# Two of the seven gate products of columns 0 to 255 placed beside the last recurrence, whose six units run in two groups of three

## The chip, the core and the metric

One core of one Trainium2 chip runs the whole program in one launch. The core has TensorE (PE; its weight loads are shown apart as PEld), VectorE (DVE), ScalarE (ACT), GpSimd (POOL) and SyncE (SP, which here only issues DMAs); 16 DMA engines move data between HBM and the on-chip memory. Time is the device time of one execution in microseconds (us); lower is better. The chip's time before is the median of three runs.

## The reference: what is computed

Two layers over 1152 tokens (1024 of one prompt, 8 times 16 of samples) of 1024 features. Layer 0 mixes tokens with an RWKV-7 recurrence, layer 1 with chunk-band attention; each is followed by a SwiGLU feed-forward network (FFN) with 2816 hidden features. Cut to what matters here:

```
mod = silu(c) @ w_ada + b_ada                    # shift, scale, gate of each sub-layer
h   = modulate(rms_norm(x, norm_mix), shift, scale)
y   = recurrence(r, w, k, v, a, b)               # per head, a 64x64 state, token after token
x   = x + gate * ((y_normed * g) @ w_o)          # output projection
h   = modulate(rms_norm(x, norm_ffn), shift, scale)
x   = x + gate * ((silu(h @ w_gate) * (h @ w_up)) @ w_down)
```

All matrices are float32. The kernel splits each float32 operand into a high and a low part and multiplies high by high, high by low and low by high, three matmuls in place of one.

## The kernel before, in words

**Layout.** Features lie on the 128 partitions, tokens along the free axis. The 1152 tokens are three blocks of 384 (b = 0, 1, 2) in layer 0's mixer and two column groups in the FFN: c = 0 is columns 0 to 511, c = 1 columns 512 to 1151.

**The mixer's stages.** The projections of block b run beside the recurrence of block b-1. The recurrence is cut into nine windows of 128 tokens, each in two halves of the heads (hf = 0, 1): 18 units. `win_prep` (L875) loads a unit's operands and forms its small products, `win_run` carries the state, `win_y` (L1065) and `win_post` (L1108) form, normalise and store its output. `windows` (L1192) takes the units in pairs: it prepares a pair, weaves the two state chains step by step, finishes both, prepares the next pair.

**The last recurrence.** In `layer0a` (L1271) the six units of windows 6, 7 and 8 run, in three pairs, beside a second stream, `early`: the output projection of block 0 (`outproj(0)`) in turn with the rest of the modulation vectors (`self.ada`, weights `in_wada`), then `outproj(1)`. Both load 128x1024 weight tiles named raw on POOL's DMA queue (L318), from a ring of two buffers here. An output projection has eight units, one for each row tile of 128 features: a raw tile of `in_rw_o` is split by ACT into whi (L330) and by DVE into wlo (L331), 24 matmuls of 384 columns go into the bank acc, and DVE adds the residual into e (L1228). Its block's rms is known after the eighth unit. The operand of a block, yg, is loaded and split into 16 mx tiles through mr, a ring of two. The windows' memory (pool `win`) is given back only after the last unit; the FFN's first buffers then take its place.

**The FFN of layer 0.** It forms gate and up together by a Strassen-Winograd scheme: for each of the 22 row tiles f of 128 hidden features, seven products (0, 1, 2, 4, 5, 6, 3 in this order) of 128x512 weight combinations with half of the features (512) of half of the columns of a group. `strassen_in` (L1344) makes the seven operands of a group: it loads x and the rms, normalises (L411, L412), combines (L1357), splits (L330, L331, tiles h). Products 0 and 1 are the gate weights as they are, times the two feature halves of the group's first columns: their sum is the plain gate of columns 0 to 255 (c = 0) and 512 to 831 (c = 1). `gate_up` (L1408): a product is 12 matmuls of 256 columns (c = 0) and 12 of 320 (c = 1) into one of three PSUM banks (S, S, PT); product 0 is copied to t1 by ACT (L1430), product 1 is added to it by DVE into s0, ACT takes Silu of s0 (L1432); products 2 and 4 are copied by ACT (L1433, L1434), and three additions of each f run on POOL (L1427 on POOL). t1 also enters the sums of product 5. The weight combinations are four POOL additions per f (L1398 to L1401), and POOL also adds down-projection weights (L1516 to L1519). Group c = 0 of f = 0 runs alone, then the operands of c = 1 are made, then c = 1 of f = 0, then f = 1 to 21 with both groups.

**What sets the order.** The program is written as interleaved generators; a scheduler with its own cost model then sets the order on every engine and queue before the launch. So each engine works through a fixed list, and what stands behind a waiting instruction on its engine waits too.

## Time and profile before

| what | us |
|---|---|
| median of three runs (lowest, highest) | 3768.5 (3764.55, 3778.86) |
| the profiled execution | 3766.23 |
| its span | 3764.4 |
| TensorE busy in the span | 3441.4 (91%) |
| output projection of block 0 with the modulation, from its first result to its last | 1023 to 1146 |
| output projection of block 1, first result to last | 1163 to 1200 |
| first result of the output projection of block 2 | 1247 |
| first f of the FFN with both groups | 1332 |

The page gives busy time by engine, then the span in 40 slices (each digit is a tenth; PEclk is the granted TensorE clock in tenths), then the chain of work that ended last, then groups of instructions. A matmul's duration there is that of one in flight; since they overlap, its price in a dense stretch is the distance between starts.

### The profile page before, as it was taken

Reading aid. Unit: us, or ns where it says so; the run is one execution under the profiler, and the core shown is the slowest. Engines: PE = TensorE matmul, PEld = TensorE weight load, DVE = VectorE, ACT = ScalarE, POOL = GpSimd, SP = SyncE. Lnnn points to the kernel's source line nnn. Section 1 sums busy time; section 2 is a strip of 40 time slices with the busy share of each in tenths; the row PEclk is TensorE's granted clock in tenths of the full one; section 3 lists DMA queues with packets and bytes.
Section 4 is the critical chain, followed back from the end, with each engine's and each line's share of the span. In section 5 each row is a group of like instructions: output and inputs, shape, how many; then the busy total and the mean of one; then the engine's idle time right before and its main releaser. Section 6 shows DMA issues by size and latency. Waiting matters only on the chain.

```text
span 3764.4 us, 74445 instructions
## 1 busy us (share of the span) xinstructions
PE 3441.4 (91%) x28982; PEld 3083.1 (82%) x28982; DVE 2248.7 (60%) x4366; ACT 1660.0 (44%) x3176; POOL 787.5 (21%) x775
## 2 busy tenths in 40 slices
PE   5888999999889799999999889789889899999999
PEld 4677778777667699999888869677667789999999
DVE  4667676765446765555446742666675675665655
ACT  5545556554223533333334542555564443333442
POOL 0000000000011066676100000000000146766200
PEclk9888899889699899999999999899999899999999
DMA  5776776677666444444889422445465434444764
GB/s 212 231 223 162 202 222 191 191 205 208 174 199 203 141 129 141 140 138 153 272 295 329 145 72 80 136 140 161 149 206 170 156 109 141 142 149 143 235 211 158
DMA packets 545938, 664.65 MB, mean 177 GB/s; under 512 B 137232, under 2 KB 405520, under 8 KB 541104
## 3 DMA queue, kind: packets, MB, share of 16 engines
q1 hardware_dynamic: 468736, 556.44, 46.5%
q0 software_dynamic: 23760, 85.08, 7.4%
q10 hardware_dynamic: 53088, 18.36, 2.1%
q8 instruction: 228, 3.74, 0.4%
q14 instruction: 126, 1.03, 0.1%
HBM read 483.18 MB, written 176.53 MB: 175 GB/s over the span
## 4 chain that ended last, share of the span: by engine, by line
PE 67%; DMA 13%; DVE 9%; issue 5%; ACT 4%; SPq 1%; POOL 1%; ACTq 0%; DVEq 0%; POOLq 0%
PE S L145 30%; PE PT L145 15%; PE acc L145 12%; PE st L145 3%; PE O L145 2%; PE G L145 1%; PE PT L2107 1%; PE aux L145 1%; DVE h L331 1%; PE Y L145 1%; DMA TT<-Z 1%; DMA raw<-in_wada 1%; DVE wlo L331 1%; DMA raw<-in_rw_o 1%; DMA aw<-in_wadb 1%
## 5 line engine op out<-in xcount | busy, mean ns | idle before, releaser
L145 PE MATMUL S<-h,w 128*128 128x256 f32 (+1 forms) x7374 | 1032.5, 299 | 24.8 <-ACT h L330 7.2
L145 PEld LDWEIGHTS S<-h,w 128*128 128x128 f32 x7374 | 1002.2, 191 | 43.2 <-issue 15.3
L330 ACT ACTIVATE w<-rq 128x512 fp32r<-128x512 f32 (+1 forms) x500 | 304.0, 614 | 645.8 <-PE S L145 259.6
L145 PE MATMUL acc<-mx,whi 128*128 128x384 f32 x1728 | 510.8, 373 | 31.6 <-ACT mx L330 12.3
L145 PE MATMUL PT<-h,w 128*128 128x256 f32 (+1 forms) x3714 | 527.4, 298 | 9.5 <-DVE h L331 3.5
L331 DVE TENSOR_TENSOR w<-rq,w 128x512 fp32r<-128x512 f32 (+1 forms) x500 | 384.7, 774 | 251.0 <-ACT w L330 212.6
L145 PEld LDWEIGHTS PT<-h,w 128*128 128x128 f32 x3714 | 505.3, 190 | 16.2 <-issue 6.5
L145 PEld LDWEIGHTS acc<-mx,whi 128*128 128x128 f32 x1728 | 339.7, 205 | 61.7 <-ACT mx L330 15.4
L145 PE MATMUL acc<-mx,wlo 128*128 128x384 f32 x864 | 318.0, 368 | 8.2 <-DVE wlo L331 8.2
L1427 POOL TENSOR_TENSOR t<-t,t 128x576 f32<-128x576 f32 (+1 forms) x132 | 221.9, 1683 | 263.0 <-ACT t L1434 153.3
L331 DVE TENSOR_TENSOR h<-h,h 128x1024 fp32r<-128x1024 f32 (+6 forms) x152 | 169.3, 1127 | 133.5 <-ACT h L330 120.6
L330 ACT ACTIVATE h<-h 128x1024 fp32r<-128x1024 f32 (+6 forms) x152 | 142.5, 950 | 158.8 <-DMA h<-bd 120.4
L145 PEld LDWEIGHTS acc<-mx,wlo 128*128 128x128 f32 x864 | 177.0, 205 | 19.7 <-DVE wlo L331 12.3
L331 DVE TENSOR_TENSOR wlo<-raw,whi 128x1024 fp32r<-128x1024 f32 x114 | 139.1, 1222 | 82.3 <-ACT whi L330 81.5
L330 ACT ACTIVATE whi<-raw 128x1024 fp32r<-128x1024 f32 x114 | 119.7, 1053 | 129.9 <-PE acc L145 73.0
L145 PE MATMUL S<-h,wh 128*128 128x320 f32 (+1 forms) x744 | 146.7, 351 | 19.5 <-ACT xo L1794 10.0
L145 PEld LDWEIGHTS S<-h,wh 128*128 128x128 f32 x744 | 123.6, 196 | 39.3 <-ACT xo L1794 15.8
L1427 DVE TENSOR_TENSOR t<-S,t 128x576 f32<-128x576 f32 (+1 forms) x117 | 86.7, 741 | 113.7 <-PE S L145 113.7
L145 PE MATMUL acc<-h,wh 128*128 128x256 f32 (+1 forms) x864 | 133.8, 303 | 3.5 <-DVE ht L391 1.3
L145 PEld LDWEIGHTS acc<-h,wh 128*128 128x128 f32 x864 | 118.0, 194 | 11.5 <-DVE ht L391 3.4
L1357 POOL TENSOR_TENSOR h<-h,h 128x256 f32<-128x256 f32 x12 | 10.7, 918 | 540.3 <-PE PT L145 540.3
L2108 ACT ACTIVATE pts<-PT 128x640 f32<-128x640 f32 (+4 forms) x128 | 72.6, 567 | 88.0 <-PE PT L2107 73.7
(480 smaller groups left out, 5536.4 us busy)
## 6 DMA issues: line engine op xcount, KB each, us to landing
bd<-t SPq DMA_DIRECT2D x154, 160.0 KB, 1.9
rq<-in_wg SPq DMA_DIRECT2D x88, 256.0 KB, 3.0
rq<-in_wu SPq DMA_DIRECT2D x88, 256.0 KB, 2.6
ws<-in_wd SPq DMA_DIRECT2D x64, 352.0 KB, 3.5
ws<-ws SPq DMA_DIRECT2D x64, 352.0 KB, 3.1
bd<-t SPq DMA_DIRECT2D x152, 128.0 KB, 1.8
rq<-ws SPq DMA_DIRECT2D x72, 256.0 KB, 3.2
h<-bd SPq DMA_DIRECT2D x28, 640.0 KB, 6.8
```

What stands on the lines that cost most here:

```text
L145: return nc.tensor.matmul(out, lhsT, rhs, start=start, stop=stop)
L330: self.nc.scalar.activation(hi, x, AF.Copy)
L331: self.nc.vector.tensor_tensor(lo, x, hi, ALU.subtract)
L1357: gp.tensor_tensor(out[j], x[j], y[j], op)
L1427: return eng.tensor_tensor(out, x, y, ALU.add)
L2107: nc.tensor.transpose(pt[:, j * 128:(j + 1) * 128], P[:, j * 128:(j + 1) * 128], self.C("ident"))
L2108: nc.scalar.activation(pts[:, 0:nk * 128], pt[:, 0:nk * 128], AF.Copy)
```

## The change

Products 0 and 1 of group c = 0 are computed earlier, beside the last recurrence, for all 22 f. `first_in` loads columns 0 to 255 of block 0's new x, normalises them with the rms that `outproj(0)` has just made, and splits them into eight high and eight low tiles, which lie in buffers that the recurrence no longer uses (pa, Aab, t11, p1, L, T, stmp, and a new one, op). `first_gates` loads the plain gate weights `in_wg0[f]` whole (128x1024, on POOL's queue), splits them, runs 24 matmuls of 256 columns in two halves of a bank acc, copies the first half by ACT, adds the second by DVE (L1310 in the changed kernel), and stores both, product 0 and the sum of 0 and 1, to gd in HBM. `gate_up` then loads those 256 columns of t1 and s0 from gd, and runs products 0 and 1 for the other 320 columns alone; `strassen_in` leaves out the splits of operands 0 and 1 of c = 0.

Beside this, the six units of the last recurrence run in two groups of three (12 13 16, then 14 15 17, as window and half in the base 2), the ring of raw has three buffers there in place of two, three steps of `early` are written for one of `windows` in place of two, the mix tiles are 384 wide in place of 408, and some operands of single units lie in other pools.

```diff
-        self.T = self.wp.tile([128, 16, 16], F32, name="T")
+        self.T = self.wt("T", [128, 16, 16])
...
-        ring, nr = (self.st, 1) if (w, hf) == (7, 1) and 1 else (self.wt, 3)
+        ring, nr = self.wt, 3
-        bk = self.wt("BK", [128, 8, 2, 64], 1)
+        bk = (self.st if (w, hf) in ((6, 1), (7, 0), (8, 1)) else self.wt)("BK", [128, 8, 2, 64], 1)
...
-    def windows(self, us):
+    def windows(self, us, n=2):
-        pairs = [us[i:i + 2] for i in range(0, len(us), 2)]
+        pairs = [us[i:i + n] for i in range(0, len(us), n)]
-                if u is run[0]:
+                if u is not run[-1]:
...
-            nc.sync.dma_start(self.rr[:, cols], self.sq_done(st))
+            self.rms = self.sq_done(st)
+            nc.sync.dma_start(self.rr[:, cols], self.rms)
...
+    def first_in(self):
+        wt = lambda tag, shape, bufs=1: self.wt(tag, shape, bufs, F32R)
+        p = wt("pa", [128, 2, 8, 64]).rearrange("p a b c -> p (a b c)")
+        t = [p[:, 256 * i:256 * i + 256] for i in range(4)]
+        for _ in range(2):
+            q = wt("Aab", [128, 8, 64], 2).rearrange("p a b -> p (a b)")
+            t += [q[:, 0:256], q[:, 256:512]]
+        t += [wt(f"{n}{h}", [128, 8, 32]).rearrange("p a b -> p (a b)") for n in ("t11", "p1") for h in range(2)]
+        t += [wt(n, [128, 16, 16]).rearrange("p a b -> p (a b)") for n in "LT"] + [wt("stmp", [128, 256])]
+        t.append(self.st("op", [128, 256], 1, F32R))
+        self.op = t[0:8], t[8:16]
+        self.Af0 = self.gain("nf0", 32)
+        for f in range(8):
+            x = self.mraw()[:, 0:256]
+            self.nc.sync.dma_start(x, self.x1[:, f, 0:256])
+            self.normed(x, self.rms[:, 0:256], self.Af0, 24, f)
+            self.split(self.op[0][f], self.op[1][f], x)
+            yield
+    def first_gates(self):
+        nc = self.nc
+        hi, lo = self.op
+        last = None
+        for f in range(22):
+            wh, wl = self.wunit(self.pp, self.a["wg0"][f])
+            if last:
+                nc.sync.dma_start(*last)
+            pz = self.bank("acc", 2)
+            t = self.st("gr", [128, 512], 3)
+            for h in range(2):
+                z = pz[:, 256 * h:256 * h + 256]
+                for k in range(4 * h, 4 * h + 4):
+                    s = slice(k * 128, (k + 1) * 128)
+                    self.mm3(z, wh[:, s], wl[:, s], hi[k], lo[k], k % 4 == 0, k % 4 == 3)
+                if h:
+                    nc.vector.tensor_tensor(t[:, 256:512], z, t[:, 0:256], ALU.add)
+                else:
+                    nc.scalar.activation(t[:, 0:256], z, AF.Copy)
+                yield
+            last = self.gd[:, f], t
+        nc.sync.dma_start(*last)
...
-        self.nraw, self.nhi, self.nlo = (2, 2, 2)
-        self.nmix, self.nmr = 16, 2
+        self.nraw, self.nhi, self.nlo = (3, 2, 2)
+        self.nmix, self.nmr, self.wmix = 16, 2, TB
         def early():
             yield from self.alternate(self.outproj(0), self.ada, 1, 1)
-            yield from self.outproj(1)
+            yield from self.first_in()
+            yield from self.alternate(self.outproj(1), self.first_gates(), 1, 2)
             self.last_in()
-        for _ in self.alternate(self.windows([divmod(int(x), 2) for x in '12 13 16 14 15 17'.split()]), early(), 1, 2):
+        for _ in self.alternate(self.windows([divmod(int(x), 2) for x in '12 13 16 14 15 17'.split()], 3), early(), 1, 3):
...
         def product(i):
             hi, lo = next(W)
+            ccs = [c for c in cs if c or not a or i > 1]
+            if not ccs:
+                return None
             t = self.wide()[:, 256:832]
-            for c in cs:
+            for c in ccs:
...
-        nc.scalar.activation(t1, product(0), AF.Copy)
-        add(dve, s0, product(1), t1)
+        if a:
+            nc.sync.dma_start(t1[:, 0:256], gd[:, 0:256])
+            nc.sync.dma_start(s0[:, 0:256], gd[:, 256:512])
+        z = product(0)
+        if n1 > a:
+            nc.scalar.activation(t1[:, a:], z[:, a:], AF.Copy)
+        z = product(1)
+        if n1 > a:
+            add(dve, s0[:, a:], z[:, a:], t1[:, a:])
```

In `gate_up`, `a` is 256 for layer 0 where group c = 0 takes part, and 0 elsewhere.

**How the order moves: POOL's DMA queue in the last recurrence.** Before, from the end of the first output projection on (raw is the ring, in_wada the modulation's weights, in_rw_o the output projection's):

```order
L318 DMA raw_12344<-in_rw_o 128x1024
L318 DMA raw_12360<-in_wada 128x1024
L318 DMA raw_12375<-in_wada 128x1024
L318 DMA raw_12566<-in_rw_o 128x1024
L318 DMA raw_12647<-in_rw_o 128x1024
L318 DMA raw_12814<-in_rw_o 128x1024
L318 DMA raw_12970<-in_rw_o 128x1024
```

Now, in the same place (in_wg is the gate weight of one f):

```order
L318 DMA raw_12197<-in_rw_o 128x1024
L318 DMA raw_12213<-in_wada 128x1024
L318 DMA raw_12233<-in_wada 128x1024
L318 DMA raw_12608<-in_rw_o 128x1024
L318 DMA raw_12624<-in_wg 128x1024
L318 DMA raw_12731<-in_wg 128x1024
L318 DMA raw_12909<-in_wg 128x1024
L318 DMA raw_12944<-in_rw_o 128x1024
L318 DMA raw_12960<-in_wg 128x1024
L318 DMA raw_13054<-in_wg 128x1024
L318 DMA raw_13153<-in_wg 128x1024
L318 DMA raw_13188<-in_rw_o 128x1024
```

The second output projection's eight loads, which followed one another, now stand three gate loads apart: 30 loads in the place of eight.

**DVE at the end of the last recurrence.** Before, the last unit's normalisation (tile y, L1134) and the splits of its output into the operand mx come just ahead of the FFN's first normalised tile (x, L411) and of the first result e of the output projection of block 2:

```order
L1134 SCALAR_TENSOR_TENSOR y_13546<-y_13546,par,bv_13544 128x128 x4
L1135 TENSOR_TENSOR y_13546<-y_13546,gl_13542 128x512
L331 TENSOR_TENSOR mx_13419<-y_13546,mx_13418 128x128
L331 TENSOR_TENSOR mx_13425<-y_13546,mx_13424 128x128
L331 TENSOR_TENSOR mx_13431<-y_13546,mx_13430 128x128
L331 TENSOR_TENSOR mx_13437<-y_13546,mx_13436 128x128
L411 SCALAR_TENSOR_TENSOR x_13581<-x_13581,mod,x_13580 128x512
L411 SCALAR_TENSOR_TENSOR x_13582<-x_13582,mod,x_13580 128x512
L411 SCALAR_TENSOR_TENSOR x_13583<-x_13583,mod,x_13580 128x512
L1228 SCALAR_TENSOR_TENSOR e_2379_13733<-acc_13706,mod,rr_13731 128x256
```

Now the last unit's normalisation (L1135 in the changed kernel) stands here, with gates (gr, L1310) and output-projection units still to come; eight gate sums and three results e of block 1 stand between it and the first e of block 2:

```order
L1135 SCALAR_TENSOR_TENSOR y_14368<-y_14368,par,bv_14366 128x128 x4
L1136 TENSOR_TENSOR y_14368<-y_14368,gl_14364 128x512
L1310 TENSOR_TENSOR gr_13772<-acc_13771,gr_13772 128x256
L331 TENSOR_TENSOR wlo_13818<-raw_13815,whi_13817 128x1024
L1229 SCALAR_TENSOR_TENSOR e_2401_13907<-acc_13805,mod,rr_13905 128x384
L331 TENSOR_TENSOR wlo_13867<-raw_13864,whi_13866 128x1024
L369 TENSOR_TENSOR sqa_12777<-sqa_12777,kk_13910 128x384
L1310 TENSOR_TENSOR gr_13823<-acc_13822,gr_13823 128x256
L331 TENSOR_TENSOR wlo_13922<-raw_13919,whi_13921 128x1024
L1310 TENSOR_TENSOR gr_13872<-acc_13871,gr_13872 128x256
```

The end of this stage is no longer the last unit's output but the last gates.

**SP's queue at the FFN's first loads.** Before, the rms of block 1 is stored (rr) eight rows ahead of the load of the FFN's rms and x (x from rr, then x from the residual stream):

```order
L1266 DMA rr<-rms_13386 128x384
L1047 DMA out_wkv_s<-s_2264_13127 128x256
L1047 DMA out_wkv_s<-s_2268_13138 128x256
L1047 DMA out_wkv_s<-s_2280_13190 128x256
L1047 DMA out_wkv_s<-s_2284_13201 128x256
L1190 DMA out_wkv_p<-S_2289_13237 128x256
L1047 DMA out_wkv_s<-s_2293_13247 128x256
L1047 DMA out_wkv_s<-s_2297_13258 128x256
L1744 DMA x_13580<-rr 128x512
L1351 DMA x_13581<-x_108 128x512
```

Now the rms is stored behind the last gates' store, and the load follows it closely:

```order
L1315 DMA gd<-gr_14170 128x512
L1441 DMA rq_14566<-in_wg 128x512
L1441 DMA rq_14568<-in_wg 128x512
L1441 DMA rq_14570<-in_wu 128x512
L1441 DMA rq_14572<-in_wu 128x512
L1268 DMA rr<-rms_14375 128x384
L1574 DMA ws_15527<-in_wd 128x4x176
L1574 DMA ws_15750<-in_wd 128x4x176
L1263 DMA x_108<-e_2505_14543 128x384
L1260 DMA rr_14638<-in_x 128x384
L1804 DMA x_14410<-rr 128x512
L1399 DMA x_14411<-x_108 128x512
```

The FFN's first operands now wait for an rms that is made at the very end of the stage.

More of the change, by code (lines that the diff above doesn't have):

```diff
@@ L561 @@
     nmix = 16
+    wmix = 408
     nsq = 1
@@ L1342, in feats, with strassen_in @@
         return [t[f // 2][:, f % 2 * w:(f % 2 + 1) * w] for f in range(8)]
-    def strassen_in(self, B, x, r, A, sh0, c, X, gp=None):
+    def strassen_in(self, B, x, r, A, sh0, c, X, gp=None, skip=()):
         nc = self.nc
         n = (256, 320)[c]
-        B[c] = [[self.slot(c, F32R).rearrange("p (k t) -> p k t", k=4) for _ in range(2)] for _ in range(7)]
+        B[c] = [[self.slot(c, F32R).rearrange("p (k t) -> p k t", k=4) for _ in range(2)] if i not in skip else None for i in range(7)]
         gp = gp or nc.gpsimd
@@ L1352, in strassen_in @@
         b11, b12, b21, b22 = ([X[4 * h + j][:, o:o + n] for j in range(4)] for h in range(2) for o in (0, n))
-        put = lambda i, t: [self.split(B[c][i][0][:, j], B[c][i][1][:, j], t[j]) for j in range(4)]
+        put = lambda i, t: [self.split(B[c][i][0][:, j], B[c][i][1][:, j], t[j]) for j in range(4) if B[c][i]]
         def comb(out, x, y, op):
@@ L1412, in gate_up @@
         gp = nc.gpsimd
+        a = 256 if gd is not None and cs[0] == 0 else 0
         n0, n1 = 256 * cs[0], 576 if cs[-1] else 256
@@ L1449, in ffn @@
         spill = self.down_open(l)
-        self.gate_up(spill(0), B, iter(W), (0,))
+        gd = lambda f: None if l else self.gd[:, f]
+        self.gate_up(spill(0), B, iter(W), (0,), gd(0))
         for _ in part1:
@@ L1734, in dense @@
                 self.wq_open(c2, "0")
-                A = self.gain("nf0", 32)
+                A = self.Af0
                 B, HK, X = {}, {}, {}
```

9 lines of the change are left out of this document (5 added, 4 removed).

## The prediction

> **What bounds the kernel now.** I read the page, then the stretches that the change touches, then the chain of waits in the last recurrence.
>
> ```profile
> PE 3441.4 (91%) x28982; PEld 3083.1 (82%) x28982; DVE 2248.7 (60%) x4366; ACT 1660.0 (44%) x3176; POOL 787.5 (21%) x775
> PE   5888999999889799999999889789889899999999
> core 0: us, PE busy (x) PEld busy (x) DVE busy (x) ACT busy (x) POOL busy (x), PEclk, DMA share, GB/s
> 1018.00:1148.00 130.00, 119.15 (x1382) 89.86 (x1384) 58.42 (x131) 35.66 (x66) 13.95 (x28) 0.92 0.68 200
> 1148.00:1200.00 52.00, 49.54 (x453) 44.80 (x451) 29.59 (x51) 21.67 (x37) 5.79 (x11) 0.93 0.66 203
> 1200.00:1247.00 47.00, 38.62 (x391) 25.58 (x387) 27.91 (x74) 16.31 (x38) 4.83 (x9) 0.85 0.54 173
> 1247.00:1331.00 84.00, 62.73 (x314) 57.01 (x312) 77.63 (x188) 51.13 (x107) 10.15 (x8) 0.84 0.34 109
> 1331.00:1770.00 439.00, 438.80 (x3297) 438.69 (x3298) 260.12 (x302) 144.89 (x241) 302.36 (x252) 1.00 0.45 143
> ```
>
> The five stretches are: the output projection of block 0 with the modulation, that of block 1, the last pair's end, the step into the FFN, and the FFN. In the FFN (1331 on) TensorE is busy 438.80 of 439 at full clock: what is taken off it there comes off the time. In the last recurrence "busy" flatters it: 1382 matmuls take 130 us, 94 ns each on average, at a clock below 1, and the engines behind it are busy less than half the time. The step into the FFN is DVE's (77.63 of 84).
>
> **The FFN: what is removed.**
>
> ```profile
> 1504.15 3.36 PE L145 MATMUL PT<-h,w 128*128 128x256 f32 x24
> 1507.34 6.55 PE L145 MATMUL S<-h,w 128*128 128x256 f32 x48
> 1513.73 3.36 PE L145 MATMUL PT<-h,w 128*128 128x256 f32 x24
> 1293.57 5.46 PE L145 MATMUL S<-h,w 128*128 128x256 f32 x24 [2.47 <-DVE kk L391]
> 1298.83 1.67 PE L145 MATMUL PT<-h,w 128*128 128x256 f32 x12
> 1300.33 3.04 PE L145 MATMUL S<-h,w 128*128 128x256 f32 x24
> 1303.21 1.60 PE L145 MATMUL PT<-h,w 128*128 128x256 f32 x12
> 1304.65 3.37 PE L145 MATMUL S<-h,w 128*128 128x256 f32 x24
> ```
>
> Three products of both groups start at 1504.15 and end where the next starts, at 1513.73: 3.19 us each, 22.4 us for an f. The second half of the rows is c = 0 alone: twelve matmuls of 256 columns take 1304.65 - 1303.21 = 1.44 us, 120 ns each. Each of f = 1 to 21 loses two such dozens, 2.88 us: 21 x 2.88 = **60.5 us less**. Nothing replaces them on TensorE. The copy and the sum shrink, and two loads of 128 KB per f are added on SP; their landing has the time of products 2 and 4 before t1 is read, so I cost them at nothing; were they late by a product, it would be 3.2 us an f.
>
> f = 0 loses its first 24 matmuls, which ran cold: 1298.83 - 1293.57 = 5.26 us. But that stretch is DVE's, and the next group will be the cold one. Between 0 and 5.3 us; I take **2 less**, near the DVE bound.
>
> **The step into the FFN.**
>
> ```profile
> L331 DVE TENSOR_TENSOR h<-x,h 128x256 fp32r<-128x256 f32 x28 | 10.6, 415 | 0.0
> rr<-rms SPq DMA_DIRECT2D x2, 192.0 KB, 1.9
> x<-rr SPq DMA_DIRECT2D x1, 256.0 KB, 3.0
> x<-x SPq DMA_DIRECT2D x8, 256.0 KB, 4.9
> ```
>
> Eight of the 28 splits go: 8 x 0.415 = **3.3 us less** on DVE, the engine that decides there. Against that, the FFN's rms and x are now loaded right after block 1's rms, which is made at the stage's end: store 1.9, load 3.0, x 4.9. Before, they were there when the last unit ended. All of it bare would be 9.8; DVE has block 2's weight splits and residuals meanwhile, so 0 to 8, and I take **5 more**.
>
> **The last recurrence: what is added.** First what paces it.
>
> ```profile
> 1040.04 5.90 DMA raw<-in_wada
> 1057.36 4.67 DMA raw<-in_rw_o
> 1078.26 5.38 DMA raw<-in_rw_o
> 1086.31 3.73 DMA raw<-in_wada
> 1094.46 4.11 DMA raw<-in_rw_o
> 1106.43 5.54 DMA raw<-in_wada
> POOL raw L318 <- PE aux L145: 64.0, 18, 8.8
> POOL raw L318 <- DVE wlo L331: 19.5, 4, 6.4
> 1145.34 0.62 DVE L1228 SCALAR_TENSOR_TENSOR e<-acc,mod,rr 128x384 f32<-128x384 f32 x1 [2.98 <-PE acc L145]
> 1163.21 0.61 DVE L1228 SCALAR_TENSOR_TENSOR e<-acc,mod,rr 128x384 f32<-128x384 f32 x1
> 1199.61 0.61 DVE L1228 SCALAR_TENSOR_TENSOR e<-acc,mod,rr 128x384 f32<-128x384 f32 x1
> 1246.93 0.48 DVE L1228 SCALAR_TENSOR_TENSOR e<-acc,mod,rr 128x256 f32<-128x256 f32 x1 [2.58 <-PE acc L145]
> ```
>
> The first six rows are all the weight loads on the chain between 1040 and 1148: 29.3 us in which the chain waited for a landing. The two waits below say why: POOL's queue stood 64.0 and 19.5 us because both raw buffers were in use. A third buffer issues each load one place earlier. That is worth 0 (PE's fixed list binds anyway) to 29.3; I take **20 less**, nearer the upper end since the landings themselves are on the chain. The last four rows are residual results: block 0 ends at 1145.34, block 1 runs from 1163.21 to 1199.61, block 2's first is at 1246.93.
>
> ```profile
> 1141.55 3.92 DMA mr<-yg
> L145 PE MATMUL acc<-mx,whi 128*128 128x384 f32 x160 | 46.7, 368 | 6.0 <-ACT mx L330 5.3 <-ACT whi L330 0.6
> L331 DVE TENSOR_TENSOR wlo<-raw,whi 128x1024 fp32r<-128x1024 f32 x10 | 12.2, 1224 | 3.7 <-ACT whi L330 3.7
> L330 ACT ACTIVATE whi<-raw 128x1024 fp32r<-128x1024 f32 x11 | 11.6, 1056 | 18.7 <-PE acc L145 16.0 <-DMA raw<-in_rw_o 2.7
> L331 DVE TENSOR_TENSOR mx<-mr,mx 128x384 fp32r<-128x384 f32 x8 | 4.4, 553 | 3.9 <-ACT mx L330 3.9
> raw<-in_rw_o POOLq DMA_DIRECT2D x12, 512.0 KB, 4.2
> ```
>
> Then `first_in`: eight loads through mr, a ring of two, ahead of block 1's eight through the same ring. The first two are loaded early; three rounds follow, each a load (3.92) and the normalisation and split of two tiles (about 0.5 each): 5 us. 3 x 5 = **15 more** (8 if the smaller tiles land faster, 20 with the rms and PE's list behind it).
>
> Then 22 gates and eight units together. After the first of each, 21 gates and 7 units remain. A unit took (1199.61 - 1163.21) / 7 = 5.2 us beside the windows. A gate's 24 matmuls are 2.88 at full clock. 7 x 5.2 + 21 x 2.88 = 96.9 us, the lower bound, with what the last units of the recurrence needed after 1200 absorbed. The upper bound is that every weight load keeps the pace of 5.2: 28 x 5.2 = 146. A raw buffer is held for a landing of 4.2 and splits of 1.06 and 1.22, some 7 us, so three allow a load every 2.3: the loads don't bind unless landings double. ACT and DVE have 28 x 1.06 and 28 x 1.22 = 34 us, far from the bound. I take 112: the lower end, and 15 for the last units' waits in PE's list. Before, the same point (block 1's first result to block 2's first) took 1246.93 - 1163.21 = 83.7. So **28 more** (13 to 62). The windows in threes end before the gates by the order on DVE, so their own length no longer counts.
>
> **The sum**, on the profiled execution's 3766.2 (span 3764.4; 2.3 below the median of the runs): -60.5 - 2 - 3.3 + 5 - 20 + 15 + 28 = -38, **3728 us**. The recurrence ends 23 later, the FFN is 60 shorter.
>
> **A rule on the clock.** In the trace, 24 matmuls after an idle stretch took 5.26 us and the next 24 took 2.88, and the granted clock is 0.92 and 0.93 in the stretches that take the gates. The Trainium skill, TensorE: Matmul & The Clock Gate, Part 1, says that an idle window of some 3.4 us halves the clock and a busy one restores it. The trace agrees; by that rule denser work raises the clock here, which the sum leaves out, and were all 528 moved matmuls cold they would cost 528 x (219 - 120) ns = 52 us more.
>
> **Rivals.**
>
> *A: POOL becomes the FFN's bound.*
>
> ```profile
> L1427 POOL TENSOR_TENSOR t<-t,t 128x576 f32<-128x576 f32 x46 | 76.8, 1671 | 81.1 <-DVE t L1427 40.7 <-ACT t L1434 40.4
> L330 ACT ACTIVATE w<-rq 128x512 fp32r<-128x512 f32 x109 | 68.7, 630 | 179.2 <-PE S L145 67.2 <-POOL rq L1401 41.1 <-issue 36.0
> ```
>
> POOL works 302.36 of 439 us, 15.4 per f of 22.4. These rows are from 350 us, 15.6 f: POOL waits 2.6 per f for ACT's copy of product 4, and ACT in turn 2.6 for POOL's last weight sum, a loop. 15.4 + 2.6 = 18.0 fits in the new 19.5. If the other wait, 2.6 for DVE's sum after product 5, stays as it is, 20.6 doesn't: an f then gains 1.8, 21 x 1.1 = 23 us less gain, 3751. For it: the loop is real. Against: that wait shrinks as POOL runs late, and TensorE has no idle time to show for either wait now. The Trainium skill, GPSIMD Engine Reference, section 1, says that POOL shares its SBUF interfaces with VectorE and contends with two-input instructions; by that rule a DVE that works more densely in the shorter f would stretch POOL's part too. No row here shows it apart.
>
> *B: the other side.* The loads keep the pace of 5.2 us in both halves, because PE's fixed list mixes units and gates and each late landing holds everything behind it: the third buffer gives nothing (0) and 28 pieces take 146 (+62). -60.5 - 2 - 3.3 + 5 + 15 + 62 = +16, 3782. It decides from 4.6 us a piece on where the third buffer gives nothing, (83.7 + 45.8) / 28, and from 5.3 where it gives 20. For it: 18.7 us of ACT's waits there are for landings and TensorE's bank. Against: the queue waited for buffers, of which there are more now.
>
> *C: the recurrence takes it nearly free.* Third buffer 29, `first_in` 8, 97 for the pieces, 2 for the loads: -60.5 - 2 - 3.3 + 2 - 29 + 8 + 13 = -72, 3694. For it: TensorE's real work is about half of these stretches. Against: the ends of the ranges all fall together.
>
> **How the numbers follow.** Forecast 0.60, with a range of its own from 3708 to 3750; A 0.12, B 0.12, C 0.16. This kernel's measurement tells about 0.5% from no change, 19 us: below 3750 is faster, above 3787 slower. Faster: the forecast's 0.54 and C's 0.16, 0.70. Within: the forecast's 0.06, A's 0.12 and 0.02 of B, 0.20. Slower: 0.10 of B. The range that leaves two in ten out reaches from near C to short of B: 3698 to 3772.
>
> **What would show it.** FFN: product starts 1.76 us apart for products 0 and 1 and 3.19 else, f every 19.5, TensorE still without idle; a gap ahead of the split after POOL's last weight sum would be A. Last recurrence: block 0's last residual near 1125, block 1's first near 1158, the last gate sum near 1270 and block 2's first residual with it; POOL's waits for raw buffers shrink. If block 0 still ends at 1145, the third buffer was mis-sized; if the pieces are over 4.6 us apart, B. The forecast is wrong if the stage from 1018 to block 2's first result grows by more than 45 us.

## The result and the profile after

The changed kernel takes 3829.4 us in the median of four runs (3824.5 to 3838.0), the kernel before 3767.9 beside it. The ratio on record is 1.0146, with a 95% interval of 1.0122 to 1.0170; the quotient of these two medians is 1.0163 and lies inside it. It is some 1.5% slower; 3728 was forecast, and the highest of the rivals, B, stood at 3782. The profiled execution has a span of 3823.8, 59.4 more than before.

The page's first part, then the stretches of the changed kernel (us, busy time and instructions of PE, PEld, DVE, ACT and POOL, granted clock, DMA share, GB/s): block 0's output projection, the time up to block 1's first result, the gates beside block 1, the step into the FFN, and the FFN with f = 1 to 21.

```profile
PE 3468.0 (91%) x28982; PEld 3091.8 (81%) x28982; DVE 2289.3 (60%) x4417; ACT 1688.1 (44%) x3227; POOL 809.1 (21%) x797
1010.00:1151.00 141.00, 135.84 (x1210) 97.80 (x1210) 52.55 (x117) 31.66 (x58) 14.23 (x27) 0.79 0.63 190
1151.00:1207.00 56.00, 48.29 (x533) 37.91 (x531) 33.81 (x79) 26.75 (x56) 2.64 (x5) 0.79 0.54 143
1207.00:1343.00 136.00, 129.64 (x1073) 114.77 (x1071) 72.86 (x127) 54.81 (x91) 19.60 (x37) 0.99 0.64 204
1343.00:1412.00 69.00, 48.26 (x239) 44.01 (x240) 61.20 (x147) 42.54 (x81) 4.75 (x6) 0.82 0.50 174
1412.00:1842.00 430.00, 410.37 (x2971) 405.00 (x2971) 288.62 (x351) 154.28 (x271) 323.46 (x262) 0.99 0.52 166
```

The kernel before, cut at the same events: the units of block 1 with the windows' rest, and the FFN with f = 1 to 21.

```profile
1163.00:1247.00 84.00, 75.62 (x770) 59.48 (x769) 48.23 (x106) 29.99 (x60) 8.54 (x16) 0.92 0.57 180
1314.50:1787.00 472.50, 467.50 (x3473) 465.46 (x3474) 286.78 (x353) 159.89 (x271) 316.57 (x263) 0.99 0.44 140
```

The FFN is 42.5 us shorter, and TensorE now idles 20 us in it (430.00 - 410.37), where it idled 5 before. The gates' stretch is the loss: 136 instead of 84, with TensorE busy 129.64 of it at a clock of 0.99. The residual results that mark the stages, in the changed kernel:

```profile
1042.01 0.62 DVE L1229 SCALAR_TENSOR_TENSOR e<-acc,mod,rr 128x384 f32<-128x384 f32 x1 [5.05 <-PE acc L145]
1150.99 0.62 DVE L1229 SCALAR_TENSOR_TENSOR e<-acc,mod,rr 128x384 f32<-128x384 f32 x1 [1.47 <-PE acc L145]
1206.63 0.61 DVE L1229 SCALAR_TENSOR_TENSOR e<-acc,mod,rr 128x384 f32<-128x384 f32 x1
1327.23 0.61 DVE L1229 SCALAR_TENSOR_TENSOR e<-acc,mod,rr 128x384 f32<-128x384 f32 x1
1342.67 0.48 DVE L1229 SCALAR_TENSOR_TENSOR e<-acc,mod,rr 128x256 f32<-128x256 f32 x1 [2.54 <-PE acc L145]
```

These are block 0's first (1042.01) and last, block 1's first and last, and block 2's first. Before, block 0's last, block 1's first and block 2's first stood at 1145.34, 1163.21 and 1246.93: the delay is 6 us after block 0, 43 at block 1's first, 96 at block 2's first. The prediction's own sign of being wrong was a growth of over 45 us up to block 2's first result.

### The profile page after: what moved, and what is told of

It reads as the page before. It is cut to its first block, busy times and chain, and to the rows that moved or that the text cites. A ratio compares the mean times of both kernels' runs of the same rounds, so it can differ in the third digit from the quotient of the medians.

```text
span 3823.8 us, 74827 instructions
## 1 busy us (share of the span) xinstructions
PE 3468.0 (91%) x28982; PEld 3091.8 (81%) x28982; DVE 2289.3 (60%) x4417; ACT 1688.1 (44%) x3227; POOL 809.1 (21%) x797
## 4 chain that ended last, share of the span: by engine, by line
PE 62%; DMA 10%; DVE 10%; issue 4%; ACT 3%; SPq 1%; POOL 0%; ACTq 0%; DVEq 0%; POOLq 0%
PE S L145 28%; PE PT L145 13%; PE acc L145 11%; PE st L145 3%; PE O L145 2%; PE G L145 2%; DVE h L331 1%; DMA h<-out_kT 1%; PE PT L2167 1%; PE aux L145 1%; PE Y L145 1%; DMA TT<-Z 1%; DMA bt<-in_rel 1%; DMA h<-bd 1%; DVE w L331 0%
## 5 line engine op out<-in xcount | busy, mean ns | idle before, releaser
L145 PE MATMUL S<-h,w 128*128 128x320 f32 (+1 forms) x7113 | 1000.1, 299 | 32.8 <-DVE t L1479 8.9
L145 PEld LDWEIGHTS S<-h,w 128*128 128x128 f32 x7113 | 969.3, 191 | 51.1 <-issue 12.2
L331 DVE TENSOR_TENSOR w<-rq,w 128x512 fp32r<-128x512 f32 (+1 forms) x500 | 406.3, 818 | 322.0 <-ACT w L330 294.9
L145 PE MATMUL PT<-h,w 128*128 128x256 f32 (+1 forms) x3447 | 498.2, 299 | 13.9 <-DVE t L1479 6.8
L145 PEld LDWEIGHTS PT<-h,w 128*128 128x128 f32 x3447 | 473.8, 191 | 25.3 <-DVE t L1479 7.9
L331 DVE TENSOR_TENSOR wlo<-raw,whi 128x1024 fp32r<-128x1024 f32 x136 | 165.9, 1222 | 101.8 <-ACT whi L330 100.4
L330 ACT ACTIVATE whi<-raw 128x1024 fp32r<-128x1024 f32 x136 | 142.6, 1053 | 154.5 <-PE acc L145 95.7
L145 PE MATMUL S<-h,wh 128*128 128x320 f32 (+1 forms) x720 | 141.6, 348 | 21.9 <-ACT xo L1854 10.1
L1405 POOL TENSOR_TENSOR h<-h,h 128x256 f32<-128x256 f32 x12 | 12.1, 1029 | 560.7 <-DVE h L331 560.7
L2167 PE MATMUL PT<-cst,P 128*128 128x128 f32 x480 | 79.0, 286 | 36.4 <-ACT pts L2168 25.1
```

Source lines behind the costliest of these rows:

```text
L145: return nc.tensor.matmul(out, lhsT, rhs, start=start, stop=stop)
L330: self.nc.scalar.activation(hi, x, AF.Copy)
L331: self.nc.vector.tensor_tensor(lo, x, hi, ALU.subtract)
L1405: gp.tensor_tensor(out[j], x[j], y[j], op)
L2167: nc.tensor.transpose(pt[:, j * 128:(j + 1) * 128], P[:, j * 128:(j + 1) * 128], self.C("ident"))
```

## The experiments

Executions differ by some microseconds long before the change begins (the same matmul, TensorE's 8,701st, which lies ahead of every difference in its list, starts between 959 and 973 us). So the traces are compared by stages that start at that matmul, all read from the start of the residuals and of the FFN's first Silu of an f. "Stage" is from there to block 2's first residual, "pieces" from block 1's first to block 2's first residual, "FFN" from there to the Silu of f = 21, and "f = 1 to 21" its part after the second Silu of f = 0. (Where an expectation gives the 28 pieces as 120.6 or 98.1, that is to block 1's last residual.) In microseconds of one profiled execution each; the ratio is the one on record, against runs of the kernel before on the same chip. Differences of ratios below are between such figures; where two intervals overlap, the difference is not settled.

| kernel | ratio (95%) | stage | pieces | FFN | f = 1 to 21 |
|---|---|---|---|---|---|
| before | 1 | 287.5 | 83.7 | 539.9 | 472.4 |
| the change | 1.0146 (1.0122 to 1.0170) | 379.5 | 136.0 | 499.1 | 429.7 |
| win_only | 1.0038 (1.0018 to 1.0057) | 325.1 | 97.5 | 538.0 | 472.6 |
| ffn_only | 0.9942 (0.9921 to 0.9962) | 322.1 | 97.1 | 494.8 | 430.3 |
| in_only | 0.9933 (0.9909 to 0.9957) | 302.5 | 69.6 | 494.0 | 430.7 |
| pairs | 1.0065 (1.0041 to 1.0089) | 363.6 | 136.0 | 498.7 | 431.6 |
| gates_light | 1.0101 (1.0074 to 1.0128) | 359.5 | 111.7 | 507.4 | 438.8 |
| gates_halfw | 1.0146 (1.0108 to 1.0185) | 385.0 | 129.0 | 508.8 | 441.3 |
| raw2 | 1.0175 (1.0151 to 1.0198) | 399.9 | 148.2 | 499.4 | 430.0 |
| nhi3_raw2 | 1.0118 (1.0069 to 1.0167) | 380.8 | 132.5 | 498.8 | 430.0 |
| light_nhi3 | 1.0110 (1.0085 to 1.0136) | 369.0 | 117.9 | 508.2 | 439.0 |
| raw3_only | 0.9990 (0.9969 to 1.0010) | 288.8 | 99.0 | 537.6 | 469.6 |
| pairs_act | 1.0076 (1.0050 to 1.0102) | 360.2 | 134.8 | 503.8 | 436.1 |
| pairs_order | 1.0085 (1.0059 to 1.0112) | 366.6 | 134.9 | 505.5 | 437.3 |
| pairs_dve | 1.0083 (1.0058 to 1.0108) | 357.8 | 136.1 | 498.6 | 429.7 |
| pairs_nosum | 1.0036 (1.0018 to 1.0054) | 362.9 | 135.7 | 485.4 | 416.4 |
| few8 | 1.0024 (1.0001 to 1.0046) | 315.4 | 88.4 | 531.0 | 459.8 |
| rec_only | 1.0260 (1.0230 to 1.0290) | 386.8 | 135.0 | 549.2 | 472.2 |

### The parts one by one

**win_only**: the rest of the change without the work that it moves.

```diff
-            yield from self.first_in()
-            yield from self.alternate(self.outproj(1), self.first_gates(), 1, 2)
+            yield from iter([None] * 8)
+            yield from self.alternate(self.outproj(1), iter([None] * 44), 1, 2)
-        gd = lambda f: None if l else self.gd[:, f]
+        gd = lambda f: None
-... () if c else (0, 1))
+... ())
```

> The change with first_in and the gates left out at their places (the steps are empty, so every other instruction keeps its place) and with all seven products computed in the FFN as before: what is left of the change is the windows in threes, the third raw buffer and the pools. Theory T (the cost is the work that was added: first_in some 32 us, the gates some 52 us): within 10 us of before, 3760 to 3780, block 0 ends near 1150. Rival R (the windows in threes are what costs: three units' loads and products stand ahead of one another, and the second group begins late): 3800 or more. The prediction's term for the third buffer: 3748.

Measured: 0.38% slower, 14 us, and by the stage 37.6. Neither the 20 us of gain of the prediction nor "within 10 us" holds; what is left of the change without its work costs something by itself. Block 0's last residual comes at 199.8 us after the mark, against 185.9 before, and block 2's first another 125.3 later (101.6 before).

**ffn_only** and **in_only** keep win_only's stage, without and with first_in, and let the FFN leave out its products.

```diff
-        gd = lambda f: None if l else self.gd[:, f]
+        gd = lambda f: None if l else self.a["wg0"][f][:, 0:512]
```

> As win_only, but the FFN leaves out products 0 and 1 of columns 0 to 255 and loads 256 KB per f in their place, from an input tensor (so those two products are computed nowhere). It measures the FFN's part alone. The prediction's sum for the FFN is -61; by the trace of the change it is -44 for f = 2 to 21, with up to 9 given back at the entry: win_only minus 35 to 44. If the loads were the cause of the gap per f, the f period stays 20.35 here; if late weight splits after the recurrence were, it is nearer 19.5.

> As ffn_only, with first_in put back (eight loads of x, normalised and split) and the gates still left out. T: 20 to 32 us above ffn_only, because the eight loads go through a ring of two ahead of block 1's eight loads. R: under 10 us above ffn_only, since the windows' second group is what is waited for there. The change itself minus this run is then the cost of the gates: T 45 to 60 us, R 20 or less.

Measured: the FFN's part alone gives 0.96% (0.9942 against 1.0038), 36 us, and 43 by the traces. f = 1 to 21 takes 430.3, as in the change, so late splits out of the recurrence have no part in the missing gain (the loads from gd are there in both; pairs_nosum, below, keeps them and gets most of the gain). Without the gates first_in costs nothing: 0.9933 against 0.9942. Its chain in the changed kernel shows why (start, length, what ended last):

```profile
1153.86 10.04 DMA BK<-sp_k
1164.14 1.13 PE G L145 x8
...
1176.60 2.17 DMA mr<-x
1180.75 2.07 DMA mr<-x
1186.87 4.54 DMA mr<-yg
```

The second group of windows starts only after block 0, with loads that land at 1163.9; TensorE waits for that group in any case, and first_in's loads run beside it. It does hold back block 1: its first residual comes 49.5 us after block 0's last in in_only, 26.9 in ffn_only. But the stretch from block 1's last to block 2's first, in which the windows end, falls from 55.7 to 28.5, so the end doesn't move. In the change that stretch is 15.4 and the gates fill it; no run takes first_in out there, so its share of the loss with the gates is not known. The change against in_only is then the gates beside first_in: 1.0146 against 0.9933, 80 us; 72.6 of it from block 0's last residual to block 2's first (191.7 against 119.1), 66.5 in the pieces. Their 528 matmuls, 117 ns apart in the change and 120 in the FFN's rows, are 62 to 63. So **the gates cost the full time of their matmuls where they were put, and more**.

**rec_only**: the gates are computed in the recurrence, and the FFN does all its products as well.

```diff
-        gd = lambda f: None if l else self.gd[:, f]
+        gd = lambda f: None
```

> The change with the gates computed in the last recurrence as there, but the FFN computes all its seven products again and doesn't use them: the cost of the added part alone. By the runs so far the change is 1.46% slower and the FFN's part alone gives 0.96% (ffn_only against win_only), so if the two parts don't touch each other: +2.4%, 2.1 to 2.7. If less, the FFN's gain in the change is smaller than measured alone; the prediction had +23 us, +0.6%.

Measured: 2.60%, 98 us for the added part, stage 386.8. Less the FFN's 0.96% that makes 1.64, inside the interval of the change's 1.46. The two parts add up: the forecast had +23 and -61 for them, the runs say about +98 and -36 to -43.

### The windows in threes and the third buffer

**pairs**: the change with windows in pairs. **raw3_only**: the third buffer and the pools alone. **raw2**: the change with two raw buffers.

```diff
pairs, raw3_only:
-... split()], 3), early(), 1, 3):
+... split()], 2), early(), 1, 2):
raw3_only also: first_in and the gates out, the FFN with all products
raw2:
-        self.nraw, self.nhi, self.nlo = (3, 2, 2)
+        self.nraw, self.nhi, self.nlo = (2, 2, 2)
```

> The change with its windows in pairs and two steps of the projections to one of the windows, as before. T: within 12 us of the change, 3817 to 3841, since TensorE has the same work. R: 20 us or more below the change, 3809 or less, and block 1's first residual well before 1206.

> Of the change only the third raw buffer and the pools that make room for it: windows in pairs as before, no first_in, no gates, the FFN with all its products. The prediction's term: 20 us below before (-0.5%; its bounds 0 and -29). The difference of two and three buffers in the change, 11 us by the medians and 20 by the profiles, says -0.3 to -0.5%. Rival (the windows in threes are not what undid it, and the buffer is worth nothing without the gates): within 0.15% of before.

> The change with two raw buffers instead of three. The prediction gave the third buffer 20 us (0 to 29). By the profile of the change block 0 ended no earlier with three: if the third buffer is worth nothing there, within 8 us of the change (+1.25 to +1.7%); if it is worth what was forecast, 20 us above it (+2.0%); with 22 more loads behind the same ring it could be more, 30 us and above.

Measured: pairs is 0.81% better than the change, 30 us (16 by the stage), so rival R has a real part of the loss; win_only against raw3_only says the same, 0.48% or 18 us (36 by the stage). Both comparisons also change the steps of `early` to one of the windows, three against two, which was not taken apart. With the windows in threes, 80 us around block 0's begin look like this, in the changed kernel and then in the kernel before (clock at the third number from the end):

```profile
975.00:1055.00 80.00, 72.90 (x407) 52.80 (x405) 30.16 (x77) 13.46 (x25) 3.52 (x7) 0.52 0.57 156
```

```profile
975.00:1055.00 80.00, 71.37 (x594) 52.69 (x592) 35.57 (x89) 20.66 (x40) 5.68 (x11) 0.66 0.70 189
```

In 80 us TensorE issues 407 matmuls instead of 594, with the clock near a half. The half clock lasts 79 us on end in the change and 51 before. Over all traces it lasts 79 to 82 in six of the seven kernels with threes and three raw buffers (48 in in_only), 55 in the three with threes and two buffers, and at most 51 in all with pairs. What keeps it low for so long was not separated from the order itself.

raw3_only is no faster than before, 0.9990. Its residuals show that the buffer works and that its gain is given back:

```profile
1142.29 0.60 DVE L1229 SCALAR_TENSOR_TENSOR e<-acc,mod,rr 128x384 f32<-128x384 f32 x1
1156.34 0.62 DVE L1229 SCALAR_TENSOR_TENSOR e<-acc,mod,rr 128x384 f32<-128x384 f32 x1 [4.61 <-PE acc L145]
1198.43 0.61 DVE L1229 SCALAR_TENSOR_TENSOR e<-acc,mod,rr 128x384 f32<-128x384 f32 x1
1255.33 0.48 DVE L1229 SCALAR_TENSOR_TENSOR e<-acc,mod,rr 128x256 f32<-128x256 f32 x1 [2.26 <-PE acc L145]
```

From the mark (966.5 here, 959.5 before), block 0 ends 10.1 us earlier than before and block 1's first residual comes 13.9 earlier. But from block 1's last to block 2's first it is 56.9 us instead of 47.3, and at block 2 it is 1.4 behind. The windows have to be done by then; what projections gain by being done sooner, the windows then take alone. In the change the same buffer is worth 0.29%, 11 us, with intervals that overlap (20.5 us by the stage, of which 12.1 in the pieces, where 22 more loads pass through it).

### What a gate costs

**gates_light** computes one of four steps of each gate product (6 of 24 matmuls). **gates_halfw** loads a new weight for every second gate only. **nhi3_raw2** has three buffers for upper weight parts and two raw ones. **light_nhi3** is gates_light with those buffers.

```diff
gates_light:
-                for k in range(4 * h, 4 * h + 4):
+                for k in (4 * h,):
-                    self.mm3(..., k % 4 == 0, k % 4 == 3)
+                    self.mm3(..., True, True)
gates_halfw:
-            wh, wl = self.wunit(self.pp, self.a["wg0"][f])
+            if f % 2 == 0:
+                wh, wl = self.wunit(self.pp, self.a["wg0"][f])
nhi3_raw2:
-        self.nraw, self.nhi, self.nlo = (3, 2, 2)
+        self.nraw, self.nhi, self.nlo = (2, 3, 2)
```

> The change with 6 of the 24 matmuls of each gate in the last recurrence (the gate values are not computed in full); all 22 weight loads, splits, copies and sums stay. In the change the gates cost 72 us by the profiles (block 0's last residual to block 2's first: 191.7 against 119.1 without gates) and 1.4 to 1.5% + 0.7% by the medians, more than the 62.7 us of their matmuls at full clock. T (TensorE's list is full there, so the matmuls cost their whole time): 18 x 22 x 119 ns = 47 us below the change, so the change's +1.46% becomes +0.2%, and block 0's last residual to block 2's first takes about 145. B (loads and splits set the pace of the pieces): within 15 us of the change.

> The change with 11 weight loads and splits for the 22 gates: each odd gate uses the weights of the one before it (so its values are not the reference's); all 528 matmuls stay. T: within 12 us of the change (+1.1 to +1.8% against before). B (a load, ACT's 1.06 and DVE's 1.22 us per piece set the pace): 11 x 4 = 44 us below the change, about +0.3%.

> The change with two raw buffers and three buffers for the upper weight parts. If a piece in the last recurrence waits for the buffer of its split (ACT's 42 us of waits for TensorE in that stretch of the change), this gives back some of the 20 us that raw2 lost: +1.4% or less against before, and the 28 pieces take 125 or less. If TensorE's list alone sets the pace, it stands where raw2 stands, +1.75%, 133 us.

> The change with 6 of 24 matmuls per gate (as gates_light) and the weight rings of nhi3_raw2 (three buffers for the upper parts, two raw). The 28 pieces took 120.6 us in the change, 98.1 with 6 matmuls, 116.4 with the third split buffer. If two limits of about the same length stand side by side (TensorE's list, and the chain of split buffer, ACT's split, DVE's rest and matmuls), taking both away gives more than the sum of the two gains (27): 85 us or less. If the raw loads or the windows are a third limit, 94 to 102.

Measured: 47 us of matmuls less give 24.4 in the pieces and 0.45% of the time, half of T's forecast; from block 0's last residual to block 2's first it is 168.9, not 145. Eleven loads and splits less give 7 in the pieces and nothing in the time, which tells little here: in that execution block 0 ended 13 later after the mark and f = 1 to 21 took 11.6 more. The stretches of the pieces in gates_light, gates_halfw and in_only:

```profile
1220.00:1331.00 111.00, 96.89 (x679) 80.43 (x679) 68.75 (x119) 51.38 (x87) 19.16 (x36) 0.88 0.75 240
1229.00:1357.00 128.00, 126.73 (x1078) 113.28 (x1078) 62.28 (x118) 44.48 (x80) 14.40 (x27) 1.00 0.54 173
1199.00:1268.00 69.00, 63.08 (x565) 52.48 (x564) 43.66 (x91) 27.64 (x52) 8.56 (x16) 0.90 0.60 196
```

With half of the loads TensorE has no gap left: 126.73 of 128 us at full clock, close to the sum of in_only's 63.08 and the gates' 62 to 63. So TensorE's list alone needs some 127 us for these pieces, and the change's 136 are only some 9 above it. With a quarter of the gates' matmuls another limit takes over; the clock is also lower there, 0.88 against 0.99, which is at most 13 us of the 111 (an estimate, 0.12 of 111) and was not taken apart from that limit. ACT's splits show the second limit (busy time, mean ns of one, idle time ahead and what ended it), in the change, in gates_light, in nhi3_raw2 and in light_nhi3:

```profile
L330 ACT ACTIVATE whi<-raw 128x1024 fp32r<-128x1024 f32 x30 | 31.6, 1057 | 46.8 <-PE acc L145 42.4 <-issue 4.3
```

```profile
L330 ACT ACTIVATE whi<-raw 128x1024 fp32r<-128x1024 f32 x29 | 30.5, 1056 | 40.5 <-PE acc L145 35.2 <-issue 2.6 <-DMA raw<-in_wg 1.9
```

```profile
L330 ACT ACTIVATE whi<-raw 128x1024 fp32r<-128x1024 f32 x30 | 31.8, 1060 | 49.7 <-DMA raw<-in_wg 22.0 <-DMA raw<-in_rw_o 16.6 <-PE acc L145 7.1
```

```profile
L330 ACT ACTIVATE whi<-raw 128x1024 fp32r<-128x1024 f32 x30 | 31.8, 1059 | 48.4 <-DMA raw<-in_wg 27.2 <-DMA raw<-in_rw_o 18.2 <-DVE wlo L331 2.0
```

A split waits for its buffer until the matmuls of the piece two places ahead are done (42.4 us). With a quarter of the matmuls it still does (35.2): the piece is then a chain of buffer, ACT's split, DVE's rest and matmuls. With a third buffer the wait is 7.1, and the landings take its place (38.6), because the raw buffers are two there; the pieces still fall from raw2's 148.2 to 132.5, and the time by 0.57%. light_nhi3 takes most of TensorE's gate work and the wait for the split's buffer away and gains nothing over gates_light (117.9 against 111.7; by its expectation's measure 104.0, above the 94 to 102 for a third limit): its splits wait 45.4 us for landings, with two raw buffers and a clock of 0.86. So in the change TensorE's list is the longest limit, and close behind it stands the chain of split buffer and splits; with two raw buffers the landings join them. Three buffers of each kind were not tried.

**few8**: gates for f = 1 to 8 only, after block 1's projection, windows in pairs, and in those f the order of pairs_order (below).

```diff
-            yield from self.alternate(self.outproj(1), self.first_gates(), 1, 2)
+            yield from self.outproj(1)
+            yield from self.first_gates()
```

> Gates for f = 1 to 8 only, in the windows' tail after block 1's projection instead of beside it, windows in pairs, third buffer, and the order of pairs_order in those eight f; all other f compute their seven products in the FFN. The FFN loses 8 x 2.9 = 23 us. T (TensorE's list is not full in that tail, 38.6 us busy of 47 before at a clock of 0.85, and the third buffer gives 10 to 20): the gates cost 15 or less and the time is 0.3 to 0.7% below before. Rival (a gate costs 3 us or more wherever it stands): -0.2 to +0.2%.

Measured: 0.24% slower than before, at the edge of the rival's range and far from T's. Against raw3_only the stage is 26.6 longer, 3.3 us a gate with first_in in it, and f = 1 to 21 only 9.9 shorter, where 23 was expected.

### The FFN's missing gain

f = 1 to 21 fell by 42.7 instead of 60.5. In every second f DVE's queue and TensorE's of the changed kernel read:

```profile
1530.80 0.74 DVE L1479 TENSOR_TENSOR t<-S,t 128x576 f32<-128x576 f32 x1
1531.47 1.10 DVE L1557 TENSOR_TENSOR t<-t,t 128x576 f32<-128x576 f32 x1
...
1534.13 1.84 DVE L1559 TENSOR_TENSOR t<-t,t 128x576 f32<-128x576 f32 x1
1535.89 1.78 DVE L331 TENSOR_TENSOR w<-rq,w 128x512 fp32r<-128x512 f32 x1
1537.60 0.74 DVE L1561 TENSOR_TENSOR t<-t,t 128x576 f32<-128x576 f32 x1
1538.26 1.77 DVE L331 TENSOR_TENSOR w<-rq,w 128x512 fp32r<-128x512 f32 x1
1539.96 0.74 DVE L1564 TENSOR_TENSOR t<-t,t 128x576 f32<-128x576 f32 x1
1540.63 0.48 DVE L1479 TENSOR_TENSOR t<-S,t 128x320 f32<-128x320 f32 x1
```

```profile
1536.41 3.35 PE L145 MATMUL PT<-h,w 128*128 128x256 f32 x24
1541.16 6.66 PE L145 MATMUL S<-h,w 128*128 128x256 f32 x48 [1.40 <-DVE t L1479]
```

The four sums of lines 1557 to 1564, for the down projection, and the weight splits between them stand ahead of the sum of product 1 (1540.63), which frees the bank that TensorE then waits for. Four edits on top of pairs take it apart.

```diff
pairs_act, where a is set (in pairs_order also ahead of the sum: the copies of products 2 and 4):
-            add(dve, s0[:, a:], z[:, a:], t1[:, a:])
+            nc.scalar.activation(s0[:, a:], z[:, a:], AF.Copy)
+            add(dve, s0[:, a:], s0[:, a:], t1[:, a:])
pairs_dve:
-        add(gp, s1, s1, t5)
+        add(dve if a else gp, s1, s1, t5)
pairs_nosum, the first layer's odd f (the operands are stored without these sums):
-                nc.vector.tensor_tensor(t6, s1, e1, ALU.subtract)
-                nc.vector.tensor_tensor(e1, e1, e0, ALU.subtract)
-                nc.vector.tensor_tensor(e0, e0, t6, ALU.add)
-                nc.vector.tensor_tensor(t3, s0, e0, ALU.subtract)
```

> The pairs version, and in the FFN product 1 of columns 256 to 575 is copied out of its bank by ACT, and DVE adds from SBUF afterwards. In the change TensorE waits in every second f for DVE's sum of product 1 to free the bank (1.40 us at 1541.16), and an f takes 20.0 us where 19.4 was forecast. Theory F (that bank is all that is missing in the FFN): an f takes 19.4, 10 to 12 us less than pairs, +0.35% against before. Rival A of the prediction (POOL and ACT's loop sets the f): f stays at 20.0 and the time within 4 us of pairs (+0.65%).

> As pairs_act, and ACT's copies of products 2 and 4 stand ahead of the sum and Silu of products 0 and 1, so that no copy that frees a bank stands behind DVE. Theory F2 (TensorE waits for whichever copy stands behind DVE's sum of product 1, since DVE is full with down sums and weight splits in every second f): f = 2 to 21 takes 369 to 373 us instead of 379, 10 us below pairs, +0.4% against before. Rival A (POOL and ACT's loop sets the f at 20.0): 379 as in pairs, +0.65%.

> The pairs version with POOL's sum of products 2 and 4 moved to DVE for f = 1 to 21: POOL loses 1.5 of its 15.5 us per f, DVE gains 0.75 of its 13. Rival A of the prediction (POOL, in a loop with ACT, sets the f at 20.0 since TensorE needs only 19.4): f = 2 to 21 falls to 369 to 374 us from 379, +0.35 to +0.55% against before. D (DVE's queue, full in every second f with the sums of the down projection, sets it): 379 to 386, +0.65% or more.

> The pairs version without DVE's four sums for the down projection in every second f of the first layer's FFN (the stored operands are then not the reference's). DVE loses some 4 us per two f, POOL nothing. D: f = 2 to 21 falls to 369 to 374 us, +0.35 to +0.55%. A: 377 to 380, +0.6 to +0.7%.

Measured: f = 1 to 21 takes 431.6 in pairs, 436.1 and 437.3 in the two that free the bank by ACT, 429.7 with less work on POOL, and 416.4 with less work on DVE. (The expectations' "f = 2 to 21", from Silu to Silu, is 379.4, 383.9, 385.0, 377.7 and 373.5.) F and F2 fall: the bank is where the wait shows, and moving its release to ACT moves the wait with it (two f take 40.9 us in pairs_order, 40.7 in pairs). Differences of 8 us and more upwards in this column are not the FFN's program: gates_light, gates_halfw and light_nhi3 run the change's own and have 439 to 441, with a granted clock of 0.97 to 0.98 over f = 1 to 21 instead of 0.99. No run of that program is below 429.7, so 416.4 is outside of that. Rival A gets little from pairs_dve, though DVE took over there what POOL lost; in pairs_nosum POOL keeps its work and the gain comes, so A falls and D stands. Two f settle at 39.0 us in pairs_nosum, 19.5 each, which is the prediction's f. The stretches of pairs and of pairs_nosum:

```profile
1450.00:1830.00 380.00, 366.07 (x2687) 363.72 (x2686) 248.81 (x283) 133.29 (x229) 295.44 (x244) 1.00 0.55 171
```

```profile
1440.00:1800.00 360.00, 357.33 (x2641) 357.10 (x2640) 200.01 (x237) 131.58 (x222) 286.76 (x239) 1.00 0.57 180
```

TensorE's gap of 14 us is down to 3, with POOL as full as before and DVE 56% busy instead of 65%. DVE is far from full over the whole; in every second f it works without a break for some 10 us (1530.80 to 1541.11 in the rows above), and what TensorE waits for stands at the end of that.

## Why the prediction was wrong

**The pieces, +28 (13 to 62): wrong by size, and by the step that made the lower bound.** That step added the units at 5.2 us and the gates at 2.88, 97 in all, and took "what the last units of the recurrence needed after 1200" as absorbed. It was not: the windows' matmuls stand in the same list. Without the gates TensorE is busy 63.08 us in the pieces (in_only), the gates bring 62 to 63, and gates_halfw shows their sum as a list without a gap, 126.73 of 128 us. So the lower bound was near 127, not 97. The change took 136.0 where 112 was chosen, +52, near rival B's 146. I had read TensorE's busy time in these stretches as flattering because the matmuls are short and the other engines less than half busy. It was the truer reading: 75.62 of 84 were in use, and 22 gates filled TensorE to 129.64 of 136 at a clock of 0.99. B's pace was right (4.9 us a piece; it was said to decide from 4.6 on), its cause was not: in the change the splits wait for their buffer (42.4 of 46.8 us), and no late landing stands in their row.

**The windows in threes, "their own length no longer counts": wrong.** They were costed at nothing; the runs say 18 to 30 us by the medians, 16 to 36 by the stages. In the change, 10.5 of the 16 fall before block 0's first residual (78.8 us from the mark against 68.3 in pairs). It wasn't a term of the sum at all.

**The third buffer, -20 (0 to -29): the mechanism right, the place of its worth wrong.** Block 0 does end 10 us sooner by it. But block 2 waits for the windows, and alone the buffer brings 0.10%, no difference. I took a shorter stage for a shorter path.

**first_in, +15: not there without the gates, untested with them.** Without them it runs beside the second group's loads and first products (0.9933 against 0.9942), and the windows end last. The reckoning of three rounds of 5 us holds for the loads as a chain, which is not what ends last.

**The FFN, -60.5 - 2 - 3.3 + 5 = -61: mis-sized.** It measured -41 in the change, -43 to -44 in ffn_only and in_only. TensorE does lose 2.88 us per f: products 0 and 1 shrank from 3.19 us each to 1.76, as forecast. But TensorE passes them sooner than DVE gets through the down projection's sums and the splits of every second f. I looked only at POOL and ACT there. The missing size was near rival A's 23, and its place was another engine: f = 1 to 21 at 416.4 in pairs_nosum comes near the 411.9 that -60.5 would make. The step into the FFN came out as the sum had it, almost even: 67.4 before, 69.4 after, from block 2's first residual to the second Silu.

**The rule on POOL's interfaces**, which the Trainium skill, GPSIMD Engine Reference, section 1, gives (POOL shares its SBUF interfaces with VectorE and contends with instructions that have two SBUF inputs), shows in these traces, but by the averages it is DVE that got slower, not POOL as rival A had it. POOL's additions and DVE's weight splits in the FFN, each before and after:

```profile
L1427 POOL TENSOR_TENSOR t<-t,t 128x576 f32<-128x576 f32 x57 | 95.5, 1676 | 99.4 <-DVE t L1427 51.6 <-ACT t L1434 47.8
L1479 POOL TENSOR_TENSOR t<-t,t 128x576 f32<-128x576 f32 x57 | 87.0, 1539 | 63.6 <-ACT t L1493 50.6 <-DVE t L1479 12.2
L331 DVE TENSOR_TENSOR w<-rq,w 128x512 fp32r<-128x512 f32 x134 | 112.6, 840 | 66.4 <-ACT w L330 49.4 <-PE S L145 10.6 <-PE PT L145 6.4
L331 DVE TENSOR_TENSOR w<-rq,w 128x512 fp32r<-128x512 f32 x132 | 132.9, 1007 | 124.7 <-ACT w L330 124.7
```

POOL's additions got shorter, 1539 ns from 1676, while DVE's share rose from 0.58 (246 of 423 us) to 0.66 (249 of 379). But DVE's splits, which read two tiles in SBUF, grew from 840 ns to 1007. In the f shown above (first a split after POOL's addition, then POOL's additions beside the splits at 1535.89 and 1538.26):

```profile
1520.76 1.29 POOL L1449 TENSOR_TENSOR rq<-rq,rq 128x512 f32<-128x512 f32 x1
1522.74 0.69 DVE L331 TENSOR_TENSOR w<-rq,w 128x512 fp32r<-128x512 f32 x1 [6.88 <-ACT w L330]
1535.43 1.69 POOL L1447 TENSOR_TENSOR rq<-rq,rq 128x512 f32<-128x512 f32 x1
1537.82 1.68 POOL L1448 TENSOR_TENSOR rq<-rq,rq 128x512 f32<-128x512 f32 x1 [0.69 <-DVE w L331]
```

A split takes 0.69 us where POOL is idle and 1.78 beside POOL's weight additions, and these take 1.29 us alone and 1.69 there. DVE's sums with one operand in PSUM keep to 750 ns. So part of DVE's late stretch in every second f is time that it and POOL cost each other; how much of the missing gain that is was not tested. The prediction said that no row shows it; in the trace of before the splits already take 0.69 us with POOL idle (29 of 133) and 1.21 on average beside its weight additions (27).

**The rule on the clock** (the Trainium skill, TensorE: Matmul & The Clock Gate, Part 1) went as told in the gates' stretch: denser work, 0.99 instead of 0.92, and lighter work in gates_light, 0.88. It didn't save the stretch, since the list was full. Around block 0's begin it did not go as told: TensorE is busy for 72.90 of 80 us by the profile there, and the clock is 0.52.

**The sum, by what was measured**: +92 for the stage, -41 for the FFN, +4 each ahead of the mark and behind the FFN, which differ as much between executions of one order (the start of the mark's matmul by 14): +59. By direction the forecast failed because three terms with a total of +23 were really +92, and each had been bounded apart: the buffer's gain, the windows and the pieces all end at the same event, block 2's first result, and only one path to it counts. B, the nearest rival, had +16, with the FFN's gain in full and nothing for the windows.

## What to carry to other kernels

Work moved off an engine that is full gains only where it lands on time which that same engine leaves free: count all that stands in its list there, also the work that was to be "absorbed", before a lower bound is called one. A buffer or an overlap that ends a stage sooner is worth what the next common event gains, and that needs the other path to it. Where a stretch gets shorter, check each queue for work that had used the length of it, in the fullest period and not in the mean.

## What the runs showed of the hardware

- TensorE can be 0.9 busy by the profile and stay at half clock for 79 us on end (72.90 of 80 us at 0.52); in the kernel before it was 51, and then full clock. The length went with the order of the work: 79 to 82 in six kernels of one kind of order, with one exception (in_only, 48). Its cause is open.
- VectorE and GpSimd lengthen each other's work where both read two operands from SBUF: 128x512 splits on VectorE took 0.69 us alone and up to 1.78 beside GpSimd's 128x512 additions, and these 1.29 alone and 1.69 beside them. Sums with one operand in PSUM stayed at 0.75.
- With 204 GB/s on the queues, 512 KB weights landed in 4.6 us (in_wg in the change; 4.2 for in_rw_o before). With two raw buffers the splits then waited 38.6 us for landings (nhi3_raw2).
